# Four kinds of transfers of the mixing stage move from SyncE's queue to GpSimd's

## The chip, the cores and the metric

The kernel runs on one core of a Trainium2 chip. The metric is the device time of one execution, in microseconds; a figure for a version is the median of several executions. The engines have names of their own in the profile: PE is TensorE (PEld its weight loads), DVE is VectorE, ACT is ScalarE, POOL is GpSimd, SP is SyncE. A q behind a name (SPq, POOLq) is that engine's sequencer, which issues transfers and waits for semaphores.

## The reference, cut to what matters

One layer of a hybrid decoder, float32, for a prompt of 512 tokens and eight samples of one token each, width 1024. The two groups share all weights and are handled as 520 columns.

```
x = x + 0.5 * SwiGLU_1(rmsnorm(x))                        # d_ff 2816
h = rmsnorm(x);  z = h @ w_in                             # columns [u | q | k | v | gate_a | gate_b]
A: u -> diagonal complex SSM, 64 groups of 16 channels and 64 states -> + D u -> gelu -> sigmoid GLU
B: dilated window attention, 12 heads of 64, q and k normed per head; three head groups mixed by softmax
x = x + (sigmoid(gate_a) * A @ w_proj_a + sigmoid(gate_b) * B @ w_proj_b) @ w_out
x = x + 0.5 * SwiGLU_2(rmsnorm(x))
```

Outputs are also the SSM's last states, the new keys and values, and the samples' caches of keys and values moved on by one row.

## The kernel before

**Products.** Activations lie with channels on the 128 partitions and the 520 tokens on the columns, in two halves of 260. A weight block of 128 output channels (128 x 1024, 512 KB) is loaded by SyncE (L176) into one of two raw tiles `wr`, then split exactly into two parts: ScalarE writes the upper one (`wh`, L166), VectorE the rest (`wl`, L167), in halves of 512 columns. A product of one weight block is 8 blocks x 3 pairs of parts x 2 halves = 48 matmuls (L218, `mm`). The split runs up to three weights ahead of the products. All matmuls of products, and those of the SSM that are put between them, carry a token that fixes their order on TensorE.

**Order.** A scheduler arranges each engine's instructions by a simulation of its own; within an engine they then run strictly in order, the issues of transfers too. An issue that waits holds up what stands behind it on its engine. `dma` is SyncE's queue, `put` ScalarE's, `later` GpSimd's.

**Stages.** The first feed-forward runs to about 400 us, with the SSM's matrices made beside it; the mixing to about 835; then come the output projections and the second feed-forward. The mixing has 50 products: two blocks of queries and keys, eight blocks of `u`, ten more of queries and keys, six of values, sixteen of gates and eight of the GLU. `pace` puts a share of the other work behind each.

**The SSM in the mixing.** Each `u` block goes from PSUM through VectorE (L791, L793) into a tile `us` of four segments of 144 columns, and each segment to DRAM (`uD`, L796), where segment and channel become rows. `entry` (L665) loads a block back (`ut`, L644, two buffers), with its entry matrices (`mt<-pD`, L658, two loads, three buffers), and multiplies four pairs of groups (L672), each behind a quarter of a product. These entries begin in the fourth `u` product and need the first block then; the eighth block's are in the third product behind the `u` products. ScalarE copies the result into the states `XS` (L673). `scan` runs on VectorE (L697 to L700), and stores the last states to `out_ostate` (L724, GpSimd). `leave` (L751) loads exit matrices (`mt<-qD`) and `ut` on GpSimd, multiplies (L758 to L760), lets ScalarE copy back into `XS` (L761) and, in every second step, stores eight pieces to `yD` (L768). `y_block` loads them for the gelu (`t_G<-yD`, L1040, GpSimd).

**Norms of queries and keys.** Their 1/rms goes to DRAM (`hD`, L825); `spread` (L842) loads two rows, each repeated over 64 partitions, into one of two buffers, which lie in the attention's output tile `OB`; `normalise` (L846) multiplies on VectorE and asks for the rows two blocks on. Keys then go out on GpSimd (`out_okT`, L867).

**What else the queues hold.** SyncE also loads the samples' cached keys and values (L1061) and rows of queries (L1067). GpSimd also stores keys, values and the samples' rows, and moves the caches during the feed-forwards.

Of the kernel before, what the change touches and what calls it, by code (L numbers as in the profile page):

```python
# [21 lines left out]
NT = 520  # L22
# [6 lines left out]
CW = 144  # L29
# [5 lines left out]
# matmuls on constants in front of the first product  # L35
WARM = 2
# order of the first loads: the rows' blocks, the first two weights' halves (8..11), the third weight
# [5 lines left out]
# the scan's steps to a product of the mixing, and the products behind which the other parts' steps go:  # L43
# exit from the states, norms of queries and keys, attention, samples' scores, samples, the SSM's output
# [14 lines left out]
def build(tc, A):  # L59
# [57 lines left out]
    # what is issued inside waits for a value of the arithmetic  # L117
# [5 lines left out]
    # the moves spread over the time of the arithmetic  # L123
# [55 lines left out]
    # the first weights come in halves  # L179
# [25 lines left out]
    # the tensor engine takes these in the order given here  # L205
# [37 lines left out]
    class Norm:  # L243
# [26 lines left out]
        # a quarter of the rows on each quadrant of the partitions while 1/rms is made, then all on each,  # L270
        # through DRAM where that is soon enough
# [33 lines left out]
    def ffn(pf, xs, R, X, last_x, filler, first=(), last=False):  # L305
        first = list(first)

        # products whose rows' 1/rms is still being made leave their banks before it is there
        def product(tag, early):
            if first:  # L310
                ps = first.pop(0)
            else:
                ps = big()
                mm(ps, wnext(), xs)
            t = tmp(tag)
            if early:
                S.activation(two(t), pv(ps), AF.Copy)
                V.tensor_tensor(t, t, R, ALU.mult)
            else:
                V.tensor_tensor(two(t), pv(ps), two(R), ALU.mult)  # L320
            return t

        for pi, (m0, m1) in enumerate(PARTS):
            a = []
            for m in range(m0, m1):
                g = product("G", m < EARLY)
                s = tmp("S")
                S.activation(s, g, AF.Silu)
                u = product("T", m < EARLY)
                V.tensor_tensor(u, u, s, ALU.mult)  # L330
                a.append(split(pf, "ah", "al", u, 8))
                for _ in range(2 if m == m0 else 1):
                    move_rows(a[-1][0].bitcast(F32))
                if pi or m:
                    filler()
            for m in range(KB):
                done = pi == len(PARTS) - 1
                # the very last goes out in halves
                halves = ((0,), (1,)) if done and m == KB - 1 and last else ((0, 1),)
                w = wnext()  # L340
                for hs in halves:
                    pd, c = big(), slice(hs[0], hs[-1] + 1)
                    mm(pd, w, a, halves=hs)
                    x = two(X[m])[:, c]
                    V.scalar_tensor_tensor(x, pv(pd)[:, c], 0.5, x, op0=ALU.mult, op1=ALU.add)
                    if done:
                        last_x(m, c, x)
                if m % 2:
                    filler()

    # ================= first feed-forward, with the SSM's matrices made beside it =================
# [7 lines left out]
    # the tensor engine's clock rises with use, so it is kept busy while the first rows come  # L359
# [17 lines left out]
    # the first two products go along with the rows' arrival  # L377
# [12 lines left out]
    def ssm_build():  # L390
# [13 lines left out]
        # the skip term joins the lag kernels' first block  # L404
# [56 lines left out]
        # input factor (abar - 1) / lambda  # L461
# [47 lines left out]
        # per eight pairs of groups: entry matrices, exit matrices, lag kernels  # L509
# [5 lines left out]
        for qt in range(4):  # L515
# [15 lines left out]
            # two pairs to a transpose  # L531
# [28 lines left out]
            # a pair to each quarter of the columns  # L560
# [40 lines left out]
    # ================= mixing: one projection, then the SSM and the attention =================  # L601
# [15 lines left out]
    # queries and keys: their 1/rms comes in with the norm over each head  # L617
# [24 lines left out]
    def uload(u):  # L642
        t = smp.tile([128, 4, CW], F32, name="ut", tag="ut", bufs=2)
        later(t, uD[u])  # L644
        return t

    # block-diagonal over a pair of groups: the blocks are loaded, the zeros stay
# [16 lines left out]
    # what each chunk's input adds to the state behind it  # L664
    def entry():  # L665
        for u in range(NP // 4):
            ut, mp = uload(u), mload(pD, u, dma)
            for a in range(4):
                p = u * 4 + a
                ps = bank()  # L670
                for ri in range(2):
                    mark(T.matmul(ps[:, ri], lhsT=mp[:, a * 2 + ri], rhs=ut[:, a, 8:CW], start=True, stop=True))  # L672
                S.activation(XS[p // NH][:, :, p % NH, 9:145], ps[:, 0:2], AF.Copy)  # L673
                yield
# [3 lines left out]
    # the states in front of every chunk, for a half of the pairs: the sums of sixteen blocks of eight chunks,  # L678
    # the states in front of the blocks, then those inside
    def scan(h):  # L680
# [34 lines left out]
        # sample states  # L715
# [11 lines left out]
    # the short steps of one half go along with the wide ones of the other  # L727
# [11 lines left out]
    # a share of the scan behind every product, and of what else goes along with them  # L739
# [10 lines left out]
    # exit from the states, and the products inside a chunk  # L750
    def leave():  # L751
        for u in range(NP // 4):
# [10 lines left out]
            if u % 2 == 1:  # L763
                p = u * 4 - 4
                for g2 in range(2):
                    for t in range(4):
                        r0 = g2 * 64 + t * 16
                        dma(yD[p:p + 8, g2, :, t].rearrange("a k j -> k a j"), X[r0:r0 + 16, 0, p0 - 4:p0 + 4, 0:NC])  # L768
# [4 lines left out]
    # four segments of tokens, the samples' in front of the first and behind the last, zeros elsewhere;  # L773
    # they go to DRAM with segment and channel on the rows, two groups to a pair
# [3 lines left out]
    for m in range(KB):  # L778
# [3 lines left out]
        # the columns' halves of 260 tokens cut the third segment  # L782
# [11 lines left out]
        for s in range(4):  # L794
            o = uD[m]
            dma(bass.AP(tensor=o.tensor, offset=o.offset + s * 16 * 4 * CW, ap=[[64 * 4 * CW, 2], [CW, 64], [1, CW]]), u[:, s])  # L796
# [3 lines left out]
    # 1/rms of the rows along the partitions, in the order of the tiles and in that of all the rest  # L800
# [26 lines left out]
    # tiles of 128 tokens in their natural order; a tile's own order has every fourth token together  # L827
# [6 lines left out]
    # the first group's queries get the tokens' natural order here, its keys that of the tiles  # L834
    OB = atp.tile([128, 2, 2, 512], F32, name="OB")
    # in front of the attention its output's place serves a moved block, the norms and the samples' columns
# [5 lines left out]
    def spread(b):  # L842
        for x in range(2):
            dma(norms[b % 2][x * 64:x * 64 + 64], hD[2 * b + x:2 * b + x + 1].broadcast_to([64, NT]))
# [31 lines left out]
    # the samples' rows: to DRAM, from there to the caches  # L876
# [26 lines left out]
    # values, keys on partitions  # L903
# [24 lines left out]
    # per order of the tokens, tile and head: the negated maximum and the sum of the exponentials  # L928
# [3 lines left out]
    # the first group's queries go in the natural order, which leaves them two tiles of keys;  # L932
    # the other groups' in the order of all the rest
# [47 lines left out]
    # each order learns the other's maxima and sums; then all of a token's keys share one softmax  # L981
# [12 lines left out]
    def combine():  # L994
# [16 lines left out]
        # the values are done with, and the tokens' weights come in their place  # L1011
# [22 lines left out]
    # the SSM's output: skip term, gelu  # L1034
# [15 lines left out]
    # the samples' scores over the cached keys, beside the SSM's way out  # L1050
# [21 lines left out]
    # their softmax over all of the groups, and the values  # L1072
    def samples():
# [40 lines left out]
        # their own new rows' share  # L1114
# [4 lines left out]
        # four samples side by side, each under the weights of all of them, of which its own are kept  # L1119
# [47 lines left out]
    # gated output of the SSM branch  # L1167
# [19 lines left out]
    # the gates come back and are closed ahead of the products that they are for  # L1187
# [40 lines left out]
    # ================= second feed-forward =================  # L1228
# [27 lines left out]
# columns of a block of eight groups as (second of pair, channel, pair)  # L1256
# [97 lines left out]
```

## Time and profile before

| | |
|---|---|
| median of the runs | 1326.69 us (three runs, 1325.2 to 1327.4) |
| span of the profiled execution | 1323.7 us |
| PE busy | 1265.4 us (96%) |
| DVE busy | 755.1 us (57%) |
| ACT busy | 468.4 us (35%) |
| POOL busy | 126.7 us (10%) |
| mean granted TensorE clock | 0.981 |
| transfers on q1 (SyncE) | 145.90 MB, 36.4% of 16 engines' span |
| transfers on q0 (GpSimd) | 60.01 MB, 15.2% |

The profile is of one execution; its span runs from its first instruction to its last and is its own time as far as the profile tells it (the device time of that execution is not told apart), 3.0 us below the median of the runs. Busy time of PE is modelled at the matmuls' ends, so a busy PE is not one at its peak. Issuing a transfer counts as busy time on POOL but not on SP. GpSimd's landings are told by the profile, SyncE's only by who waits for them.

### The profile page before, as it was taken

How to read it: one execution, taken by the hardware profiler on the slowest of the kernel's cores; microseconds unless marked ns; L12 is line 12 of the kernel's file. 1: busy time of each engine (PE TensorE's matmuls, PEld its weight loads, DVE VectorE, ACT ScalarE, POOL GpSimd, SP SyncE). 2: the span in 40 equal slices, each digit the busy share in tenths (PEclk: the TensorE clock that was granted, in tenths of full speed). 3: DMA queues.
4: the chain of work that ended last, by engine and by line, in shares of the span. 5: the costliest groups of instructions: out<-in, count | busy, mean ns of one | idle time of the engine just before them, and what ended most of it. 6: DMA issues, size and time to landing. Idle time of an engine off the chain costs nothing.

```text
span 1323.7 us, 25773 instructions
## 1 busy us (share of the span) xinstructions
PE 1265.4 (96%) x10575; PEld 1240.9 (94%) x10575; DVE 755.1 (57%) x1468; ACT 468.4 (35%) x873; POOL 126.7 (10%) x211
## 2 busy tenths in 40 slices
PE   8999999999999779997679999999999999999999
PEld 7999999999999778997578899999999999999998
DVE  6794454545564239999724776776554334444442
ACT  5332233223353223342224564444333223322331
POOL 0120010001103001001221120000010001000000
PEclk9999999999999898998789999999999999999999
DMA  6665366456656445227998635546575436533332
GB/s 216 216 212 178 101 228 191 137 168 206 188 175 155 125 125 155 81 70 242 159 160 245 208 124 145 173 153 206 172 252 162 147 93 223 160 96 112 120 100 85
DMA packets 105438, 213.92 MB, mean 162 GB/s; under 512 B 45300, under 2 KB 61200, under 8 KB 104552
## 3 DMA queue, kind: packets, MB, share of 16 engines
q1 hardware_dynamic: 87064, 145.90, 36.4%
q0 software_dynamic: 7248, 60.01, 15.2%
q10 hardware_dynamic: 11008, 6.36, 2.1%
q8 instruction: 83, 1.36, 0.4%
q14 instruction: 35, 0.29, 0.1%
HBM read 188.72 MB, written 68.60 MB: 194 GB/s over the span
## 4 chain that ended last, share of the span: by engine, by line
PE 76%; DMA 11%; DVE 8%; issue 2%; SPq 1%; ACT 1%; POOL 0%; DVEq 0%; ACTq 0%; POOLq 0%
PE bigB L218 33%; PE bigA L218 28%; PE third L218 12%; DMA wr<-in_win 3%; DMA OB<-hD 2%; DVE wl L167 2%; DMA yD<-XS 2%; DMA t_G<-yD 1%; DVE t_T L698 1%; DVE t_S L697 1%; DMA mt<-qkD 1%; DMA uD<-us 1%; DVE XS L700 1%; DVE t_S L699 1%; ACT wh L166 0%
## 5 line engine op out<-in xcount | busy, mean ns | idle before, releaser
L166 ACT ACTIVATE wh<-wr 128x512 fp32r<-128x512 f32 (+2 forms) x412 | 252.7, 617 | 600.0 <-PE bigB L218 226.0
L167 DVE TENSOR_TENSOR wl<-wr,wh 128x512 fp32r<-128x512 f32 (+2 forms) x412 | 276.6, 672 | 279.6 <-ACT wh L166 275.6
L218 PE MATMUL bigB<-xh,wh 128*128 128x260 f32 (+1 forms) x1216 | 252.9, 289 | 0.3 <-ACT ks L568 0.3
L218 PE MATMUL bigB<-xh,wl 128*128 128x260 f32 (+1 forms) x1216 | 251.9, 287 | 0.0
L218 PE MATMUL bigB<-xl,wh 128*128 128x260 f32 (+1 forms) x1216 | 249.1, 286 | 0.0
L218 PEld LDWEIGHTS bigB<-xh,wl 128*128 128x128 f32 x1216 | 191.6, 191 | 2.4 <-issue 2.4
L218 PEld LDWEIGHTS bigB<-xh,wh 128*128 128x128 f32 x1216 | 190.6, 192 | 1.8 <-issue 0.8
L218 PEld LDWEIGHTS bigB<-xl,wh 128*128 128x128 f32 x1216 | 190.4, 191 | 1.1 <-issue 1.1
L218 PE MATMUL bigA<-xh,wh 128*128 128x260 f32 x704 | 143.1, 284 | 2.5 <-ACT xh L254 2.0
L218 PE MATMUL bigA<-xl,wh 128*128 128x260 f32 x704 | 142.5, 284 | 1.0 <-DVE xl L255 0.9
L218 PE MATMUL bigA<-xh,wl 128*128 128x260 f32 x704 | 142.3, 284 | 0.0
L218 PEld LDWEIGHTS bigA<-xh,wh 128*128 128x128 f32 x704 | 109.1, 190 | 4.4 <-ACT xh L254 3.4
L218 PEld LDWEIGHTS bigA<-xl,wh 128*128 128x128 f32 x704 | 108.8, 189 | 1.6 <-DVE xl L255 1.6
L218 PEld LDWEIGHTS bigA<-xh,wl 128*128 128x128 f32 x704 | 109.1, 190 | 0.2 <-DVE wl L167 0.2
L120 POOL COPY pace<-ah 1x1 f32<-1x1 f32 x48 | 36.1, 751 | 758.2 <-ACT ah L298 758.2
L218 PE MATMUL bigA<-ah,wh 128*128 128x260 f32 x352 | 71.4, 284 | 0.0
L218 PE MATMUL bigA<-al,wh 128*128 128x260 f32 x352 | 71.1, 283 | 0.0
L218 PE MATMUL bigA<-ah,wl 128*128 128x260 f32 x352 | 70.6, 282 | 0.0
L218 PE MATMUL third<-xh,wl 128*128 128x260 f32 x288 | 58.2, 283 | 0.0
L218 PE MATMUL third<-xh,wh 128*128 128x260 f32 x288 | 58.0, 282 | 0.0
L218 PE MATMUL third<-xl,wh 128*128 128x260 f32 x288 | 57.8, 282 | 0.0
L218 PEld LDWEIGHTS bigA<-ah,wh 128*128 128x128 f32 x352 | 54.2, 189 | 0.2
(384 smaller groups left out, 2038.7 us busy)
## 6 DMA issues: line engine op xcount, KB each, us to landing
out_okv<-in_kv POOLq DMA_DIRECT2D x32, 1023.5 KB, 6.3
wr<-in_wg SPq DMA_DIRECT2D x43, 512.0 KB
wr<-in_wu SPq DMA_DIRECT2D x43, 512.0 KB
wr<-in_win SPq DMA_DIRECT2D x42, 512.0 KB
wr<-in_wd SPq DMA_DIRECT2D x32, 448.0 KB
wr<-in_wd SPq DMA_DIRECT2D x16, 512.0 KB
out_okv<-in_kv POOLq DMA_DIRECT2D x8, 1022.0 KB, 5.8
ut<-uD POOLq DMA_DIRECT2D x16, 288.0 KB, 5.5
```

Source lines behind the costliest of these rows:

```text
L120: ins = G.tensor_copy(pace[0:1, 0:1], t[0:1, 0:1])
L166: S.activation(h, raw, AF.Copy)
L167: V.tensor_tensor(l, raw, h, ALU.subtract)
L218: i = T.matmul(ps[:, hf, 0:x.shape[1]], lhsT=a[:, c], rhs=x, start=k == 0 and j == 0, stop=k == n - 1 and j == 2)
L697: V.tensor_tensor(t1, w[0], x, ALU.mult)
L698: V.tensor_tensor(t2, w[1], swap(x), ALU.mult)
L699: V.tensor_tensor(t1, t1, t2, ALU.add)
L700: V.tensor_tensor(out, add, t1, ALU.add)
```

## The change

Four kinds of transfers are issued from GpSimd instead of SyncE. Their shapes, their number and what they wait for stay as they are: 16 loads of entry matrices (64 partitions x 8 pieces of 256 bytes), 32 stores of `u` (128 rows of 576 bytes each; the DRAM side's outermost dimension is 2), 32 stores of the SSM's output (16 partitions x 8 pieces of 544 bytes) and 24 broadcasts of norms (64 rows of 2080 bytes). SyncE keeps the weights, the 1/rms to DRAM, the samples' loads and the rest. The other lines of the diff take comments away and are left out here.

```
@@ entry
         for u in range(NP // 4):
-            ut, mp = uload(u), mload(pD, u, dma)
+            ut, mp = uload(u), mload(pD, u, later)
...
@@ leave
                         r0 = g2 * 64 + t * 16
-                        dma(yD[p:p + 8, g2, :, t].rearrange("a k j -> k a j"), X[r0:r0 + 16, 0, p0 - 4:p0 + 4, 0:NC])
+                        later(yD[p:p + 8, g2, :, t].rearrange("a k j -> k a j"), X[r0:r0 + 16, 0, p0 - 4:p0 + 4, 0:NC])
...
@@ the products of u
         for s in range(4):
             o = uD[m]
-            dma(bass.AP(tensor=o.tensor, offset=o.offset + s * 16 * 4 * CW, ap=[[64 * 4 * CW, 2], [CW, 64], [1, CW]]), u[:, s])
+            later(bass.AP(tensor=o.tensor, offset=o.offset + s * 16 * 4 * CW, ap=[[64 * 4 * CW, 2], [CW, 64], [1, CW]]), u[:, s])
...
@@ spread
         for x in range(2):
-            dma(norms[b % 2][x * 64:x * 64 + 64], hD[2 * b + x:2 * b + x + 1].broadcast_to([64, NT]))
+            later(norms[b % 2][x * 64:x * 64 + 64], hD[2 * b + x:2 * b + x + 1].broadcast_to([64, NT]))
```

## Rows read from the trace of the kernel before

**Rows 1.** The page's head.

```profile
span 1323.7 us, 25773 instructions
```

**Rows 2.** Stages: start:end, length, each engine's busy time (instructions), clock, DMA, GB/s.

```profile
420.00:516.00 96.00, 78.33 (x594) 75.57 (x594) 42.05 (x99) 23.66 (x53) 6.43 (x11) 0.91 0.46 135
516.00:590.00 74.00, 74.00 (x649) 71.23 (x648) 71.14 (x191) 29.74 (x61) 5.17 (x9) 1.00 0.29 84
590.00:635.00 45.00, 37.21 (x290) 36.54 (x289) 42.05 (x93) 13.07 (x30) 6.25 (x10) 0.92 0.70 202
635.00:700.00 65.00, 41.93 (x318) 40.04 (x317) 32.86 (x57) 17.62 (x40) 19.80 (x28) 0.82 0.97 171
...
850.00:1323.00 473.00, 470.54 (x3934) 470.00 (x3933) 222.21 (x352) 152.10 (x248) 23.24 (x46) 1.00 0.46 149
```

**Rows 3.** The chain that ended last, by time: start, length, what.

```profile
424.17 0.88 DVE us L791 x4
...
443.49 7.89 DMA wr<-in_win
...
845.93 5.74 PE third L218 x48
```

**Rows 4.** Timeline of SyncE's issues, 440 to 465 us.

```profile
443.49 2.54 SPq L176 DMA_DIRECT2D wr<-in_win  x1
...
446.84 6.74 SPq L796 DMA_DIRECT2D uD<-us  x4
...
457.62 7.16 SPq L796 DMA_DIRECT2D uD<-us  x4
```

**Rows 5.** Timeline of GpSimd, 455 to 515 us; in brackets idle time before.

```profile
460.86 0.54 POOL L644 DMA_DIRECT2D ut<-uD  x1 [9.65 <-DMA uD<-us]
...
507.93 1.52 POOL L658 DMA_DIRECT2D mt<-qD  x2 [2.74 <-PE s L672]
```

**Rows 6.** Issues of transfers: count, KB each, median us to landing.

```profile
ut<-uD POOLq DMA_DIRECT2D x16, 288.0 KB, 5.5
...
mt<-qD POOLq DMA_DIRECT2D x16, 192.0 KB, 5.7
...
uD<-us SPq DMA_DIRECT2D x32, 72.0 KB
...
wD<-wt POOLq DMA_DIRECT2D x1, 16.0 KB, 3.5
```

**Rows 7.** VectorE's groups by line, 420 to 516 us: busy, mean ns | idle before.

```profile
L167 DVE TENSOR_TENSOR wl<-wr,wh 128x512 fp32r<-128x512 f32 x20 | 13.7, 684 | 44.4 <-ACT wh L166 44.4
```

**Rows 8.** Timeline of TensorE: entry products, the first, two neighbours and the last.

```profile
437.08 1.25 PE L672 MATMUL s<-ut,mt 128*128 128x136 f32 x4 [5.96 <-issue]
...
446.48 0.70 PE L672 MATMUL s<-ut,mt 128*128 128x136 f32 x4
...
448.44 0.62 PE L672 MATMUL s<-ut,mt 128*128 128x136 f32 x4
...
517.36 0.62 PE L672 MATMUL s<-ut,mt 128*128 128x136 f32 x4
```

**Rows 9.** The chain again, from 594 to 700 us.

```profile
630.04 11.91 DMA OB<-hD
...
664.84 19.65 DMA t_G<-yD
```

**Rows 10.** All transfers of line 724, the stores of the last states.

```profile
DMA to landing us min/median/max: 13.7/16.7/19.3
```

**Rows 11.** Timeline of SyncE's issues: the weights about 690 us.

```profile
672.62 0.33 SPq L176 DMA_DIRECT2D wr<-in_win  x1
...
696.72 0.39 SPq L176 DMA_DIRECT2D wr<-in_win  x1
```

**Rows 12.** Timeline of TensorE, about 654 us.

```profile
654.18 0.79 PE L758 MATMUL bigB<-XS,mt 128*128 128x136 f32 x2 [9.58 <-DMA mt<-qD]
```

**Rows 13.** Timeline of GpSimd, about 650 us.

```profile
652.70 0.57 POOL L644 DMA_DIRECT2D ut<-uD  x1 [7.55 <-DMA out_ostate<-XS]
```

More of the change, by code (lines that the diff above doesn't have):

```diff
@@ L666, in entry @@
         for u in range(NP // 4):
-            ut, mp = uload(u), mload(pD, u, dma)
+            ut, mp = uload(u), mload(pD, u, later)
             for a in range(4):
@@ L767, in leave @@
                         r0 = g2 * 64 + t * 16
-                        dma(yD[p:p + 8, g2, :, t].rearrange("a k j -> k a j"), X[r0:r0 + 16, 0, p0 - 4:p0 + 4, 0:NC])
+                        later(yD[p:p + 8, g2, :, t].rearrange("a k j -> k a j"), X[r0:r0 + 16, 0, p0 - 4:p0 + 4, 0:NC])
             yield
@@ L795, in build @@
             o = uD[m]
-            dma(bass.AP(tensor=o.tensor, offset=o.offset + s * 16 * 4 * CW, ap=[[64 * 4 * CW, 2], [CW, 64], [1, CW]]), u[:, s])
+            later(bass.AP(tensor=o.tensor, offset=o.offset + s * 16 * 4 * CW, ap=[[64 * 4 * CW, 2], [CW, 64], [1, CW]]), u[:, s])
         if m > 5:
@@ L843, in spread @@
         for x in range(2):
-            dma(norms[b % 2][x * 64:x * 64 + 64], hD[2 * b + x:2 * b + x + 1].broadcast_to([64, NT]))
+            later(norms[b % 2][x * 64:x * 64 + 64], hD[2 * b + x:2 * b + x + 1].broadcast_to([64, NT]))
     def normalise(b):
```

## The prediction

> **What bounds the kernel now.** I read the table by stages first. In the second feed-forward TensorE is busy 470.54 of 473 us at full clock, so whatever the mixing gives or loses reaches the end undiminished; nothing of the change lies there [rows 1, 2]. The mixing has three poor stretches. From 420 to 516 us, while the eight u blocks are made and the entry matrices applied, TensorE is busy 78.33 of 96 us with only 594 matmuls, at a mean clock of 0.91, and no engine is near full: VectorE 42.05, ScalarE 23.66, GpSimd 6.43, the DMA engines 0.46. From 516 to 590 VectorE, with the scan, is busy 71.14 of 74 us and sets the pace. From 590 to 700 TensorE falls to 37.21 of 45 and 41.93 of 65 us, with the DMA engines at 0.70 and 0.97, though at 171 GB/s in the second part: short pieces, not bytes.
>
> Then the chain of waits: in the first stretch it runs through stores of u and through loads of weights that need 7.89 us each [rows 3]. SyncE's own timeline tells why: issuing a weight load takes 2.54 us there, and the four stores of one u block 6.74 us, the next block's beginning 457.62 - 446.84 = 10.8 us later [rows 4]. GpSimd waits for a block's stores before it loads the block back: it stands idle 9.65 us and issues, in 0.54 us, at 460.86, which is 7.3 us after SyncE was through with the stores at 453.58 [rows 4, 5]. So four stores of 72 KB each land over 7 us or more, while the one load of the same 288 KB lands in 5.5 [rows 6]; with the engines together under half busy, the stores use few of them, and weights that need all of them queue behind. VectorE's idle time before the weights' second parts is 44.4 us of those 96, all put down to ScalarE's first part, which waits for the weight [rows 7].
>
> **The change, part by part.**
> *Stores of u (32) and loads of entry matrices (16) leave SyncE.* The ceiling comes from TensorE's rows. The first entry product waits 5.96 us for u; from its start at 437.08 to that of the last at 517.36 are 31 intervals, 80.28 us. An undisturbed interval is 448.44 - 446.48 = 1.96 us, so 31 of them are 60.8. That leaves 80.3 - 60.8 = 19.5, and with the first wait 25.4 us [rows 8]. This is all that the stretch can give back.
>
> What stays: a block now goes VectorE, four stores on GpSimd (4 x 0.54 = 2.2 us, at the price of its load [rows 5]), landing, load, landing. Landing of a GpSimd store isn't shown for this size: 3.5 us for 16 KB is below it, 5.7 for a load of 192 KB in short pieces stands above; I take 4, nearer to the first, since a store is 72 KB. With 5.5 for the load [rows 6] and 0.9 for VectorE's four wide parts [rows 3], that is 12.6. The order of the matmuls leaves two whole products and a quarter, 2 x 5.74 + 1.4 = 12.9 [rows 3], for the first block, and over 15 for the others, whose products hold entries (4 x 1.96 each). So the first wait shrinks from 6 to between 0 and 2, say 1.5, and later ones vanish. I leave another 3.5 us for ScalarE and VectorE taking things in their own order. Gain 25.4 - 1.5 - 3.5 = about 20; bounds 12 (landings at 5.7 and half of the small waits left) and 25.
>
> GpSimd itself has room: seven issues a block at 0.54 to 0.76 us (the dearer is half of the 1.52 for a pair of exit loads [rows 5]) are some 4.3 us of every 7.8. Behind a wait for a block's landing it holds only the entry matrices of that block and the next block's stores, which aren't ready sooner. The gain also survives the scan: the scan is fed by the entry products, so it starts and ends earlier by the same amount, and VectorE's work after the last entry is unchanged.
>
> A page speaks against GpSimd here. VectorE is busy 42.05 of 96 us in the entry's stretch and 71.14 of 74 in the next, and the loads of u that GpSimd issues in both, sixteen with the exit's, land in 5.5 us by their median [rows 2, 6]. The Trainium skill, "DMA: Bandwidth & Descriptors", section "SWDGE vs HWDGE vs iDMA", says that GpSimd writes its descriptors into SBUF, where VectorE can lock it out in its two-port mode, while SyncE's are immune. By the trace nothing of that is seen; by the rule the loads and stores would come later by an amount that no row gives.
>
> *Norms' broadcasts (24).* They alternate with the normalising steps on VectorE over two buffers. On SyncE the last took 11.91 us to land [rows 9], amid GpSimd's stores of the samples' states, which land in 13.7 to 19.3 us [rows 10]. On GpSimd's queue the late ones go behind those same stores instead of beside them: at worst 19.3 - 11.9 = 7.4 us more, at best 2 less, since SyncE no longer holds them behind weights. Early ones are covered: VectorE is busy 42.05 of 45 us there. I take +3. Behind a late one stand, on VectorE, scan steps and the weights' second parts, and on TensorE the transposes of the samples' rows.
>
> *Stores of the SSM's output (32).* Four groups of eight, each waiting for ScalarE's copy. On SyncE the second group lies in a gap from 672.62 to 696.72 with no weight issued [rows 11]. On GpSimd eight cost 8 x 0.54 = 4.3 us, ahead of the exit's matrices and of u for the next steps; TensorE already waits 9.58 us for such a matrix at 654.18 [rows 12]. That queue is also held by transfers under way: the load of u at 652.70 waits 7.55 us for a store of states that it has nothing to do with [rows 13], and each extra transfer meets that hold sooner. Against it, weights no longer stand behind these stores. Bounds: 8 us gained (a third of the 23 that TensorE isn't busy there [rows 2]) and 2 x 9.58 = 19 lost. The rows lie nearer to a small loss, since three of the four groups come where TensorE has other products to do: +3.
>
> *Sum.* -20 + 3 + 3 = -14 us. The profiled execution's span is 1323.7 us, 3.0 below the runs' median of 1326.7; I carry the difference over to the median: 1326.7 - 14 = 1312.7, rounded to **1312 us**. If only the bounds of the terms are added, it is -25 - 2 - 8 = -35 to -12 + 7.4 + 19 = +14.
>
> **Rivals.**
> *The stores stay slow.* If the u stores run on the same few DMA engines from GpSimd too, a block still needs its 7 us and more to land, weights meet them there, and the period of 10.8 us stays. Only SyncE's issuing is relieved, by 2.54 - 0.33 = 2.2 us a weight [rows 4, 11], which the landing hides; with the 6 of the later parts the time would be about 1326.7 to 1333, say 1329. For it: the shape of the store is not changed. Against it: the same 288 KB as a GpSimd load lands in 5.5 us, and GpSimd's stores needn't share a queue with the weights.
> The page of the Trainium skill named above bears on this twice. "Issuing engines are not separate DMA queues" says that all issuers share sixteen engines and that spreading saves issue time alone, which would make this rival likely. "Why a DMA increments its semaphore by 16 and not by 1" says that the outermost dimension sets how many engines a transfer uses (here 2), with SyncE always taking the lowest and GpSimd going round, by which the rival would fall. The trace shows no single engine.
>
> *The exit pays more than the entry gains (slower).* Place: GpSimd's queue between 635 and 720 us. If each of the three groups of output stores that stand ahead of exit loads puts its 4.3 us and one landing of 5.7 between TensorE and its matrices, that is 30 us, and with 3 for the broadcasts and -20 for the entry 1326.7 + 13 = about 1340. It decides when TensorE's waits there grow by more than 17 us. For it: the queue is already held up at 652.70, and the load of y, issued at 664.84, lands 19.65 us later, with the chain behind it [rows 9]. Against it: between exit steps there are gates' products whose weights now come freely.
>
> *The exit gains too.* With weights out of the way of ScalarE's copies, a third of the 23 us comes back and the broadcasts cost nothing: 1326.7 - 20 - 8 = 1299. Against it: the long landings of the states' stores, which aren't touched, set much of that stretch.
>
> **How the numbers follow.** Forecast 0.55, stores stay slow 0.10, slower exit 0.20, gain at both ends 0.15. A difference under 0.2% (2.7 us) can't be told from none. The forecast and the last case are faster, 0.70; the slow stores split 0.06 same and 0.04 slower; slower is 0.24 with the bad exit. The likeliest case alone spans 1304 to 1322. For 8 in 10, I go down to 1297, below the double gain, and up to 1334, past the slow stores and into the milder half of the bad exit.
>
> **What would show it.** In the new profile weights from 420 to 490 us should be issued in about 0.33 us and land in 4 to 6; the first entry product should wait under 2 us; the entries should lie 2 us apart, with the last some 20 us earlier; the clock there should be granted in full. The gap on SyncE before the weight of 696.72 should be gone. The wait at 654 us for the exit's matrix tells the price of the output stores: about 13 us by my sum, over 20 by the slower rival. I am wrong if u blocks still come over ten us apart, or if the stretch from 590 to 700 us has grown by more than the first one lost.

## The result, and the profile after

The changed kernel takes 1333.49 us (median; 1333.01 to 1335.18) against 1325.95 for the kernel before: a ratio of 1.0074, with a 95% interval of 1.0051 to 1.0098. That is slower by 0.5 to 1.0%. The forecast was 1312, with a range of 1297 to 1334; the time lies at its upper edge, and on the other side of the kernel before. In what follows 0.1% is 1.3 us.

The page's head, where [rows 1] had 1323.7:

```profile
span 1331.2 us, 25769 instructions
```

The table by stages, with the columns of [rows 2]. For the fifth stage, which [rows 2] does not hold, the row of before stands in a fence of its own.

```profile
420.00:516.00 96.00, 82.61 (x658) 81.04 (x658) 49.49 (x112) 28.81 (x61) 38.89 (x53) 0.91 0.53 143
516.00:590.00 74.00, 74.00 (x647) 71.58 (x645) 73.10 (x197) 28.59 (x62) 5.29 (x10) 1.00 0.26 80
590.00:635.00 45.00, 32.45 (x258) 31.45 (x256) 42.97 (x84) 12.67 (x27) 18.95 (x32) 0.94 0.87 192
635.00:700.00 65.00, 47.54 (x351) 44.85 (x353) 26.92 (x51) 20.50 (x51) 30.94 (x50) 0.80 0.94 197
700.00:835.00 135.00, 121.88 (x1008) 112.70 (x1004) 78.65 (x135) 61.32 (x138) 22.68 (x39) 0.96 0.50 152
```

```profile
700.00:835.00 135.00, 133.12 (x1145) 123.77 (x1143) 89.72 (x151) 71.99 (x164) 19.21 (x31) 1.00 0.59 180
```

The second number of a row is TensorE's busy time, with its matmuls in brackets. From 420 to 516 us there are 64 matmuls more than before, so the entry gained, though TensorE still lacks 13 of 96 us and the clock stays at 0.91. From 590 to 635 there are 32 fewer, in the next 65 us 33 more, and from 700 to 835 there are 137 fewer. So at 700 us the changed kernel is still ahead by about what the entry gave; the gain is spent behind that, and more with it.

**The entry.** TensorE's timeline, to hold against [rows 8]: the first entry product, two later ones and the last.

```profile
437.85 1.25 PE L672 MATMUL s<-ut,mt 128*128 128x136 f32 x4 [8.18 <-DMA uD<-us]
...
465.48 0.86 PE L672 MATMUL s<-ut,mt 128*128 128x136 f32 x4 [2.69 <-DMA ut<-uD]
...
484.99 0.70 PE L672 MATMUL s<-ut,mt 128*128 128x136 f32 x4 [2.52 <-issue]
...
508.67 0.62 PE L672 MATMUL s<-ut,mt 128*128 128x136 f32 x4
```

The first still waits, 8.18 us instead of 5.96, and the entries take 508.67 - 437.85 = 70.8 us instead of 80.3. Of the ceiling of 25.4 us that is 9.5 - 2.2 = 7 us. SyncE, on the other hand, is free: its weight loads between 424 and 480 us, by their minimum, median and maximum in ns, before and now, were

```profile
L176 SPq DMA_DIRECT2D wr<-in_win x6: 1747/2227/2540, 424.4 to 474.7; - x6
```

```profile
L176 SPq DMA_DIRECT2D wr<-in_win x6: 327/328/328, 424.3 to 474.7; - x6
```

The stores of u themselves, from the view of their line (issue in ns, then the landing), and GpSimd's timeline as the first blocks pass:

```profile
L796 POOL DMA_DIRECT2D uD<-us x32: 796/808/847, 417.6 to 487.3; - x32
...
DMA to landing us min/median/max: 5.1/6.2/7.5
```

```profile
417.56 3.20 POOL L796 DMA_DIRECT2D uD<-us  x4 [0.93 <-DVE us L791]
423.33 1.58 POOL L796 DMA_DIRECT2D uD<-us  x2 [2.56 <-DVE us L791]
425.33 1.59 POOL L796 DMA_DIRECT2D uD<-us  x2 [0.42 <-issue]
429.00 1.58 POOL L796 DMA_DIRECT2D uD<-us  x2 [2.08 <-DVE us L791]
430.58 0.58 POOL L644 DMA_DIRECT2D ut<-uD  x1
```

A store costs GpSimd 0.81 us, not 0.54, and lands in 6.2 us. The first block's last store is through at 420.76, but its load, the last line, is issued at 430.58: it stands on the same queue behind the four stores of the second block and two of the third, and these wait for VectorE (the brackets of 423.33 and 429.00). It then took 7.0 us to land, so it is what ends the first wait, though the profile names a store that landed beside it. Before, with the stores on the other queue, that load went out at 431.36 as soon as they had landed, so the move brought it forward by 0.8 us only.

**The exit.** The chain of waits from 611 to 678 us, as in [rows 9]:

```profile
611.76 15.05 DMA out_ostate<-XS
...
628.46 12.44 DMA OB<-hD
...
643.35 6.26 DMA mt<-qD
...
652.10 17.09 DMA out_ostate<-XS
...
669.49 8.47 DMA t_G<-yD
```

All but 7 of these 66 us are landings of transfers from GpSimd's queue, 32 of them stores of the states, which the change does not touch. How they reach the others is seen on GpSimd's timeline (in brackets the idle time before and its releaser) and then on TensorE's, whose three longest waits from 620 to 740 us these are:

```profile
639.76 0.54 POOL L844 DMA_DIRECT2D OB<-hD  x1 [8.09 <-DMA out_ostate<-XS]
```

```profile
641.79 0.80 PE L947 MATMUL sb<-qk 64*128 64x128 f32 x4 [12.66 <-DVE qk L850]
...
686.18 3.09 PE L947 MATMUL sb<-qk 64*128 64x256 f32 x12 [8.66 <-DVE p L953]
...
710.25 2.07 PE L947 MATMUL sb<-qk 64*128 64x256 f32 x6 [6.62 <-DVE p L953]
```

A broadcast that has no use for the states waits 8.09 us for their store. It is the one before it, though, that TensorE's 12.66 us hang on: line 850 needed the broadcast issued at 628.46, and that took 12.44 us to land beside the states' stores.

This wait is not yet a loss against the kernel before, which waited 9.58 us at the same place, for the exit's matrix [rows 12], and whose first exit product came at 654.18; here it comes at 644.01. These rows part the time from 590 to 835 us at that product, first in the kernel before, then now:

```profile
590.00:654.18 64.18, 43.34 (x336) 41.98 (x335) 56.64 (x112) 17.01 (x36) 12.94 (x20) 0.85 0.79 186
654.18:835.00 180.82, 168.91 (x1412) 158.36 (x1412) 107.99 (x188) 85.67 (x197) 32.33 (x50) 0.97 0.68 180
```

```profile
590.00:644.01 54.01, 33.26 (x263) 32.00 (x261) 45.96 (x89) 12.67 (x27) 21.99 (x37) 0.87 0.89 197
644.01:835.00 190.99, 168.62 (x1349) 157.01 (x1350) 102.58 (x181) 81.82 (x188) 50.58 (x85) 0.93 0.63 164
```

Up to the product TensorE is without work for 20.8 us in both; behind it for 11.9 us before and 22.4 now. So the loss lies behind the exit's first product, where the waits of 8.66 and 6.62 us are the longest. Both end with line 953, which VectorE runs in strict order behind a round of the samples' scores (L1068), and that round waits for its rows of queries (4.71 and 5.57 us on VectorE). And on SyncE, where nothing was added, a weight comes late:

```profile
702.12 0.51 SPq L176 DMA_DIRECT2D wr<-in_win  x1
708.64 1.28 SPq L1061 DMA_DIRECT2D mt<-in_kv  x3
...
737.44 0.43 SPq L1067 DMA_DIRECT2D mt<-qkD  x1
737.91 0.43 SPq L176 DMA_DIRECT2D wr<-in_win  x1
```

Between the two weights stand four rounds of the samples' scores, each of which waits for its landing and for VectorE.

### The profile page after: what moved, and what is told of

It reads as the page before. It is cut to its first block, busy times and chain, and to the rows that moved or that the text cites. A ratio compares the mean times of both kernels' runs of the same rounds, so it can differ in the third digit from the quotient of the medians.

```text
span 1331.2 us, 25769 instructions
## 1 busy us (share of the span) xinstructions
PE 1268.5 (95%) x10575; PEld 1244.1 (93%) x10575; DVE 756.5 (57%) x1468; ACT 470.9 (35%) x873; POOL 192.8 (14%) x315
## 4 chain that ended last, share of the span: by engine, by line
PE 78%; DMA 9%; DVE 7%; issue 2%; POOL 1%; ACT 1%; SPq 0%; DVEq 0%; POOLq 0%; ACTq 0%
PE bigB L218 34%; PE bigA L218 29%; PE third L218 12%; DMA out_ostate<-XS 2%; DMA mt<-qkD 2%; DMA OB<-hD 1%; DVE wl L167 1%; DVE t_T L698 1%; DVE XS L700 1%; PE s L672 1%; DMA t_G<-yD 1%; DVE t_S L697 1%; DVE t_S L699 1%; PE sb L947 1%; DMA ut<-uD 1%
```

## The experiments

Every edit also lets the scheduler lay the order anew, so a difference of 3 us between two kernels carries little; the verdicts rest on larger ones, or on pairs that agree. The times are medians, the ratios stand against the kernel before on the same chip.

### The change in parts

Each of these makes some of the four moves and leaves the others out.

```
p_entry:  uload(u), mload(pD, u, later)      and  later(bass.AP(tensor=o.tensor, ...), u[:, s])
p_out:    later(yD[p:p + 8, g2, :, t]...)
p_norm:   later(norms[b % 2]...)
p_noout:  p_entry and p_norm
```

> Only the front half of the change: the stores of u and the loads of entry matrices go to GpSimd, the broadcasts and output stores stay on SyncE. Theory A (the entry gained 8 to 9 us and the loss arose later, from the moved output stores): the last entry product about 9 us earlier than before, and nearly all of it kept, 1316 to 1319 us. Theory B (what was gained early is lost anyway, since the later stretch is paced by the states' stores and by the samples' scores, whoever issues the rest): last entry 9 us earlier, but the end within 3 us of before.

> Only the output stores go to GpSimd. Theory A: the whole loss without the gain, 14 to 18 us slower than before (about 1341). Theory B: within 5 us of before. Rival C (the moved broadcasts make the loss): within 3 us of before.

> Only the norms' broadcasts go to GpSimd. Theory A: within 3 us of before. Rival C (late broadcasts behind the states' stores delay the transposes and all that follows): 8 to 16 us slower.

> The whole change but for the output stores, which stay on SyncE. Theory A: the entry's 8 to 9 us are kept, 1316 to 1320 us. Theory B: within 3 us of before. Rival C: slower than before by 3 to 7, as the changed kernel is.

Measured: p_entry 1320.64 us, 0.9955 [0.9935, 0.9976]; p_out 1340.65, 1.0114 [1.0083, 1.0146]; p_norm 1334.86, 1.0064 [1.0034, 1.0093]; p_noout 1328.89, 1.0017 [1.0000, 1.0035]. So the entry half gives 6 us that reach the end, the output stores alone cost 15 and the broadcasts alone 8.5. Added, that is +18; the whole change measures +10, so the two costs share some 8 us. Of the theories, B falls, since the entry's gain does reach the end, and A and C hold for a part each; p_noout, the entry's gain and the broadcasts' cost together, is where neither put it. In p_out TensorE's wait for the exit's matrix, 9.58 us in [rows 12], is little longer, and a new one of 18.44 us stands behind it, again for line 953:

```profile
654.36 0.79 PE L758 MATMUL bigB<-XS,mt 128*128 128x136 f32 x2 [10.98 <-DMA mt<-qD]
...
703.27 3.15 PE L947 MATMUL sb<-qk 64*128 64x256 f32 x12 [18.44 <-DVE p L953]
```

VectorE had stood in front of that line for a load of the samples' rows, which SyncE had issued at 666.67, 2.4 us after GpSimd issued the first of two stores of the states:

```profile
690.14 0.96 DVE L1068 TENSOR_TENSOR mt<-mt 128x768 f32<-128x768 f32 x1 [18.22 <-DMA mt<-qkD]
```

GpSimd itself waits there too. These are its waits for the states' stores from 590 to 740 us (us in total, times, longest); before, the first two were 1.9 and 7.5 us and the third was not among them.

```profile
POOL mt L658 <- DMA out_ostate<-XS: 10.2, 1, 10.2
...
POOL ut L644 <- DMA out_ostate<-XS: 8.5, 1, 8.5
...
POOL out_okv L885 <- DMA out_ostate<-XS: 6.7, 1, 6.7
```

In p_norm the longest wait is TensorE's for the normalised keys, as in the whole change, and the exit's first product follows it:

```profile
649.77 0.80 PE L947 MATMUL sb<-qk 64*128 64x128 f32 x4 [11.99 <-DVE qk L850]
650.82 0.79 PE L758 MATMUL bigB<-XS,mt 128*128 128x136 f32 x2 [0.25 <-DMA mt<-qD]
```

Here too that product comes earlier than before, by 3.4 us, so what the broadcasts cost is lost behind it; no single wait there stands out as its place.

### Which wait carries the loss: SyncE's order, the samples' rows, or the states' stores

Three edits of the changed kernel. The first gives SyncE's weights and scores a fixed order:

```
-        dma(raw[:, 0:n], ap)
+        tc.stamp_issue_order_token(dma(raw[:, 0:n], ap).ins, "loads")
...
-            dma(t[:, g * 256:(g + 1) * 256], src)
+            i = dma(t[:, g * 256:(g + 1) * 256], src)
+            if kv == 0:
+                tc.stamp_issue_order_token(i.ins, "loads")
...
-            dma(qb, sampled[0][b:b + 1].broadcast_to([128, 768]))
+            tc.stamp_issue_order_token(dma(qb, sampled[0][b:b + 1].broadcast_to([128, 768])).ins, "loads")
```

> The changed kernel, with the order of two kinds of loads on SyncE written out: weights and the samples' loads for their scores are put into the order of the program's text, so that no weight stands behind more than two rounds of scores (in the changed kernel the weight issued at 737.91 us stands behind four). Theory Q (what the changed kernel loses between 700 and 740 us is the order on SyncE that the scheduler arrived at): that weight is issued about 720 us, and the time falls from 1333.5 to 1315 to 1322. Theory T (the samples' rows reach DRAM late, behind the stores of the states on GpSimd's queue, and everything behind them waits): weights still wait for the rounds of scores, 1330 to 1338.

The second takes one store away from behind the states:

```
-        later((qkD, vD)[x].rearrange("s (b f) -> (s b) f", f=128), o)
+        (put if x == 0 else later)((qkD, vD)[x].rearrange("s (b f) -> (s b) f", f=128), o)
```

> The changed kernel, but the store of the samples' rows of queries and keys is issued from ScalarE's queue, so that it doesn't go behind the stores of the states on GpSimd's. Theory T (that store lands in 16.2 us instead of 6.2 and delays the samples' scores, and with them the weights behind them on SyncE): it lands in under 8 us, the first round of scores is 10 us earlier, and the time falls to 1318 to 1325. Theory Q (order on SyncE decides): it depends on the order that comes out; if weights still stand behind four rounds the time stays over 1328.

The third makes the states' stores short:

```
+        o9 = smp.tile([128, 2, NH, 9], F32, name="o9", tag="o9", bufs=1)
         for ri in range(2):
-            later(A["ostate"][ri][:, pr], X[:, ri, :, 136:145])
+            V.tensor_copy(o9[:, ri], X[:, ri, :, 136:145])
+            later(A["ostate"][ri][:, pr], o9[:, ri])
```

> The changed kernel, with the last states first copied by VectorE into a compact tile, so that their four stores run in rows of 576 bytes on the SBUF side instead of pieces of 36 bytes. Theory S (these stores hold the DMA engines for 13 to 19 us each, and whatever GpSimd's queue has behind them pays; the moved stores and broadcasts lose there): the stores land in under 8 us, the transfers behind them in 5 to 8, and the time falls by 12 to 20 us, to 1314 to 1321. Theory Q or T alone: the stores land faster, and the time falls by under 6 us.

Measured: a_order 1325.15 us, 1.0005 [0.9990, 1.0019]; a_tok 1332.68, 1.0067 [1.0049, 1.0085]; a_ost 1307.73, 0.9881 [0.9863, 0.9899].

The order on SyncE is worth 8 to 9 us of the changed kernel's time; that is short of the 11 to 18 that its theory asked for, and the weight in question went out at 733.48, not at 720. The late store of the samples' rows falls as a cause: it landed in 8.7 us instead of 16.2, and the load for the first round of scores went out at 662.6 instead of 672.2, yet the time stayed. That load itself was slow, as VectorE's wait for it shows, and TensorE again waited for line 953 behind the rounds:

```profile
675.26 0.96 DVE L1068 TENSOR_TENSOR mt<-mt 128x768 f32<-128x768 f32 x1 [11.00 <-DMA mt<-qkD]
```

```profile
696.29 2.07 PE L947 MATMUL sb<-qk 64*128 64x256 f32 x6 [12.55 <-DVE p L953]
```

Short stores of the states give 26 us, more than the 12 to 20 expected. Their landing (11.8/15.7/17.1 us in the changed kernel) and the stage from 635 to 700 us:

```profile
DMA to landing us min/median/max: 3.2/3.7/6.8
```

```profile
635.00:700.00 65.00, 59.58 (x444) 54.72 (x443) 38.33 (x67) 28.27 (x74) 28.15 (x49) 0.90 0.80 228
```

444 matmuls instead of 351, and neither the wait of 12.66 nor that of 8.66 us is left on TensorE's timeline; the longest there is 5.19. The same four stores move the same 288 KB; only the pieces on the SBUF side grew, from 36 to 576 bytes. Other queues gain too: of ScalarE's stores of gates (`gD`, L874), three have landings that the profile tells, 7.1, 14.4 and 16.7 us in the changed kernel and 5.4, 6.5 and 7.1 here.

### Is it the moves, or the states' stores that they stand beside?

The same edit of the states on the kernel before, on the entry half, and on each exit move alone.

```
b_ost:   before  + compact states
pe_ost:  p_entry + compact states
po_ost:  p_out   + compact states
pn_ost:  p_norm  + compact states
```

> The kernel before, with the last states copied into a compact tile ahead of their stores, so that these run in rows of 576 bytes; none of the four moves. It gives what the change costs once these stores are short: the changed kernel with them is at 1307.7. Theory S (output stores and broadcasts lose on GpSimd only because of what the states' stores do to that queue): without them the change is worth its entry half alone, 5 to 8 us, so this kernel comes to 1312 to 1316. Theory X (the two moves also cost through the order and the issues on GpSimd's queue): this kernel is as fast as the changed one with short stores or faster, 1298 to 1308.

> Stores of u and loads of entry matrices on GpSimd, output stores and broadcasts on SyncE, states stored through the compact tile. Against the changed kernel with the compact tile (1307.7) it tells what the two exit moves cost there. Theory S: within 3 us of it, 1304 to 1311. Theory X: the exit moves still cost some 10 us, so 1294 to 1300.

> The kernel before with the output stores alone on GpSimd (+15 us where the states go out in pieces of 36 bytes), and with states through the compact tile. Theory S (the stores lose only beside those pieces): within 4 us of the kernel before with the compact tile (1314.8), 1310 to 1319. Theory X (they lose by their issues and their place on GpSimd's queue): 10 us or more above it, over 1324.

> The kernel before with the broadcasts alone on GpSimd (+8.5 us where the states go out in pieces), and with states through the compact tile. Theory S: within 4 us of 1314.8, 1310 to 1319. Theory X: over 1320.

Measured: b_ost 1314.80 us, 0.9907 [0.9874, 0.9940]; pe_ost 1306.78, 0.9863 [0.9842, 0.9883]; po_ost 1311.76, 0.9866 [0.9846, 0.9886]; pn_ost 1310.11, 0.9852 [0.9833, 0.9872]. In a table, each move's effect beside the two kinds of state stores, as differences of ratios:

| | pieces of 36 bytes | rows of 576 bytes |
|---|---|---|
| entry half | -0.45% | -0.44% (pe_ost - b_ost) |
| output stores alone | +1.14% | -0.41% (po_ost - b_ost) |
| broadcasts alone | +0.64% | -0.55% (pn_ost - b_ost) |
| both exit moves on top of the entry half | +1.19% (after - p_entry) | +0.18% (a_ost - pe_ost) |

All four lie where theory S put them, and X falls. The entry half doesn't care. Both exit moves together cost 1.2% beside the pieces and nothing that can be told without them. Alone they cost nothing there either; the runs of b_ost spread from 1306.0 to 1318.4 us, so that the small gains in the second column are good to about 0.4%. The kernel before gains 0.9% too when its states go out in rows; the change had made that old fault dearer.

### Why the entry gave 7 us of its 25: shape or queue

Each store of u in two of 64 partitions; on the changed kernel with `later`, on the kernel before with `dma`:

```
-            later(bass.AP(..., ap=[[64 * 4 * CW, 2], [CW, 64], [1, CW]]), u[:, s])
+            for h in range(2):
+                later(bass.AP(tensor=o.tensor, offset=o.offset + (h * 64 + s * 16) * 4 * CW, ap=[[CW, 64], [1, CW]]), u[h * 64:h * 64 + 64, s])
```

> The changed kernel, with each store of u cut into two of 64 partitions, whose outermost dimension is 64 instead of 2: 64 issues on GpSimd instead of 32. Theory E (a store with an outermost dimension of 2 runs on two of the sixteen engines, and that keeps the stores slow from GpSimd too): the stores land in 3 to 4 us instead of 5 to 7.5, u comes a product earlier, the first entry product waits under 4 us, and the time is 4 to 8 us below the changed kernel's, 1326 to 1330. Theory I (GpSimd's time to issue is what a block costs there, 0.8 us each): twice the issues make a block's stores 2 to 3 us later, the first wait grows, and the time is 1334 to 1340.

> The kernel before with each store of u cut into two of 64 partitions, on SyncE, and nothing else. Theory E (shape, not queue): the entry's stretch goes as in the kernel with both repairs, TensorE is busy for 94 us or more of 420 to 516, and of the ceiling of 25.4 us some 15 to 27 reach the end: 1299 to 1311. If what is gained is lost to the pieces of the states behind it, as it was in the changed kernel: 1312 to 1322.

Measured: a_half 1319.02 us, 0.9968 [0.9950, 0.9987]; b_half 1302.77, 0.9801 [0.9783, 0.9819]. On the kernel before, with nothing moved, the new shape gives 26 us. For b_half, these are the stage from 420 to 516 us, the first entry product and the last, and the stores' own line (issue in ns, landing in us; on SyncE the landings of 16 of the 64 stores are told):

```profile
420.00:516.00 96.00, 96.00 (x829) 93.94 (x827) 67.31 (x158) 35.21 (x72) 11.71 (x20) 1.00 0.58 160
```

```profile
430.34 0.62 PE L672 MATMUL s<-ut,mt 128*128 128x136 f32 x4
...
490.39 0.62 PE L672 MATMUL s<-ut,mt 128*128 128x136 f32 x4
```

```profile
L797 SPq DMA_DIRECT2D uD<-us x64: 445/590/1601, 418.1 to 473.3; - x64
...
DMA to landing us min/median/max: 1.8/3.0/5.4
```

TensorE is never without work, at full clock, and the entries take 60.05 us, where the prediction counts 60.8 for 31 undisturbed intervals. Theory E holds, and it was the shape and not the queue that made the ceiling. The changed kernel with the same cut lands its stores in the same 3.0 us and gains 14, more than the 4 to 8 expected, but half of what the kernel before gains. Theory I falls: twice the issues (0.53 us each instead of 0.81) did not make the kernel slower. The first load still goes out behind the next blocks' stores, and TensorE still waits:

```profile
429.43 2.11 POOL L797 DMA_DIRECT2D uD<-us  x4 [2.50 <-DVE us L791]
431.52 0.58 POOL L644 DMA_DIRECT2D ut<-uD  x1
```

```profile
434.83 1.25 PE L672 MATMUL s<-ut,mt 128*128 128x136 f32 x4 [5.76 <-DMA ut<-uD]
```

In b_half that load went out 6.4 us earlier:

```profile
425.13 0.57 POOL L644 DMA_DIRECT2D ut<-uD  x1 [11.46 <-DMA uD<-us]
```

### Both repairs, and the square of the two halves of the change

```
b_oh:   before  + compact states + cut stores of u (all transfers where they were)
pe_oh:  b_oh + entry half on GpSimd
x_oh:   b_oh + output stores and broadcasts on GpSimd
a_oh:   the changed kernel + both repairs (all four moves)
```

> The changed kernel with both repairs: compact states and each store of u in two of 64 partitions. Their gains lie in different stretches (25.9 us after 600 us, 14.4 before), so if they add, 1331.5 - 25.9 - 14.4 = 1291, range 1289 to 1296. If what the entry gains is lost again at a later wait, 1300 to 1308.

> The kernel before with both repairs and none of the moves: the stores of u stay on SyncE, in 64 issues. Theory E (the u stores were slow by their shape, whichever queue issues them): a weight is issued in 0.33 us in the entry's stretch here too, the entry gains 12 to 18 us, and the time is within 4 us of the changed kernel with both repairs, 1288 to 1299. Theory N (the queue that the weights share is what costs): it stays 8 us or more above that kernel, over 1299.

> The entry half of the change with both repairs. Between the unchanged kernel with both (1287.9) and the changed one with both (1295.3). Theory G (64 issues at 0.8 us on GpSimd, and a block's load and entry matrices behind them, are what the entry pays there): 1294 to 1298. Theory O (the difference is the exit half's): 1286 to 1290.

> Both repairs, with output stores and broadcasts on GpSimd and the entry's transfers on SyncE: the last corner of the square. Theory S (the exit half costs nothing beside short stores): the ratio is within 0.003 of the kernel before with both repairs (0.9713), so 0.968 to 0.974, some 1284 to 1291 us. Theory X (a cost of its own in a tighter schedule): 0.976 or more.

Measured: b_oh 1287.88 us, 0.9713 [0.9698, 0.9727]; pe_oh 1298.97, 0.9780 [0.9754, 0.9807]; a_oh 1295.29, 0.9769 [0.9753, 0.9786]; x_oh 1284.35, 0.9687 [0.9664, 0.9709].

In the kernel before and in the changed one, where each repair was also run alone, the two add up nearly in full, and b_oh is at the low end of what theory E gave it. With the stores cut, the entry half, which had given 0.45%, costs 0.67% (pe_oh - b_oh) and 0.82% (a_oh - x_oh): 9 to 11 us. That is theory G's side, with pe_oh 1 us above its range; its price of 0.8 us an issue does not hold, for a cut store takes 0.53. What remains of G is the place on the queue: the first load goes out at 432.84 in pe_oh and at 425.07 in b_oh, and TensorE is busy for 87.83 us of 420 to 516 there, against 96.00. The exit half gives 0.11% (a_oh - pe_oh) and 0.26% (x_oh - b_oh), within what can be told from nothing. So two small edits beside the change are worth 38 us to the kernel before, and its entry half is best left out. x_oh is the fastest, 42 us below the kernel before, though its interval meets that of b_oh.

## Why the prediction was wrong

**The ceiling was right, the gain was not.** Of the 25.4 us read from [rows 8] I took 20, with 12 as the lower bound; the trace shows 7, the runs 6. The ceiling itself held: b_half gave 26. What failed is the step "What stays". Of the 13 us that are short, 6.7 are the first wait (8.18 us instead of 1.5) and 6.5 the entries behind it, which took 10.0 us more than the undisturbed 60.8 instead of the 3.5 that I left for them: 5.2 in the waits of 2.69 and 2.52 us, the rest at a clock of 0.92. For the first wait, three terms were too small: 0.54 us to issue a store (0.81; [rows 5] showed a load), 4 us to land it (6.2, above my bound of 5.7), and the first load, for which I counted landing alone, stood behind six stores on its new queue until 430.58. That last one is the step that I waved through with "the next block's stores, which aren't ready sooner": they are not ready, and the load behind them waits with them. For the entries I had named only ScalarE's and VectorE's own order; b_half, where they take 60.05 us with cut stores on SyncE, shows that most of it hung on the stores.

**The cause was named, and given 0.10.** In "The stores stay slow" I wrote that the blocks would need as long from GpSimd if the stores ran on few DMA engines there too. It did not come whole: blocks of stores went out some 7.7 us apart (447.02, 454.76, 462.38 on GpSimd's timeline) and not 10.8. But the landing it spoke of stayed long. I argued against it from the load of the same 288 KB, which lands in 5.5 us [rows 6]; but that load has another shape. The cut stores tell shape from queue: from either queue they land in a median of 3.0 us, against 6.2 from GpSimd uncut. No row shows how many DMA engines a store used. The Trainium skill, "DMA: Bandwidth & Descriptors", section "Why a DMA increments its semaphore by 16 and not by 1", has the slowest dimension set that number; by its rule the cut takes it from 2 to 16, and the traces agree so far as they show it, by the landings. Its section "Issuing engines are not separate DMA queues", by which spreading saves the time of issuing alone, fits too: SyncE's 2.23 us for a weight became 0.33, and 6 us reached the end.

**The exit's two terms of +3 were +8.5 and +15.** Alone, the broadcasts cost more than my upper bound of 7.4, the output stores lay inside theirs of 19. The step that failed is the path. I priced the output stores by TensorE's wait for the exit's matrix, and placed them near a small loss since it has other products then; but that wait is not where they are paid (10.98 us in p_out, 1.41 in the whole change). They are paid in VectorE's strict order: a round of the samples' scores waits for its rows, line 953 stands behind it, and TensorE waits for that, 18.44 us in p_out, 8.66 and 6.62 in the whole change. My sum has no term for the rounds of scores. The sum of the terms as measured alone is -6 + 8.5 + 15 = +18, the whole is +10: on top of the other three moves the output stores cost 7.6 us (after - p_noout) and not 15, so the two exit costs are in part the same.

**The slower rival came true in place and sign, at another price and by another cause.** I gave it 0.20 and 1340 us, as 30 us of issues and landings between TensorE and its matrices. The loss fell in that stretch, but on VectorE's order and not as issues in front of the exit's matrices, and it was 1.2% or 16 us; issues cost nothing that can be told, since the same moves beside short stores of the states are free. The row that mattered was in front of me, [rows 10], with the load held at 652.70 [rows 13] beside it: I took the states' stores for a background that "set much of that stretch", and asked for the broadcasts alone what a transfer pays beside them.

**What I said would show it.** Weights were issued in 0.33 us, as forecast. The first wait under 2 us and the full clock in the entry did not come, the last entry was 8.7 us earlier and not 20, and SyncE still has a gap between two weights, from 677.87 to 702.12. The wait at 654 us was to tell the price of the output stores, and told nothing. Nor did my sign of being wrong: from 590 to 700 us TensorE is without work for 30.9 us before and 30.0 now, and the loss came behind.

**Still open.** Whether the pieces delay other transfers more by holding up GpSimd's issues (8.09 us at 639.76) or by slowing what is under way (a broadcast landing in 12.44): both are in the rows, and no run parts them. The slowing is not GpSimd's alone: ScalarE's stores of gates took 14.4 and 16.7 us beside the pieces, and the load that p_out waits 18.22 us for was SyncE's. Why the pieces cost more once the exit's transfers are GpSimd's is therefore open. Of the loss, 8 us come back with another order on SyncE alone; how much of it would remain an effect of the states' stores was not tried.

## What to carry to other kernels

Before transfers are moved to another queue, look at what lands slowly and why: a store's shape can be the whole of its price, and then it takes that price along. A queue that holds a group of slow transfers can charge it to those that join while it is under way, so the price of a move is read from the slowest landing on the new queue and not from the time of an issue, and then from what stands in order behind whoever waits for it. And a load that was free to go as soon as its data had landed loses that freedom when the next block's stores come to stand ahead of it.

## What the runs showed of the hardware

- Four stores of 72 KB with SBUF pieces of 36 bytes landed in 11.8 to 17.1 us (13.7 to 19.3 before) and took GpSimd 1.18 us each to issue; as rows of 576 bytes they landed in 3.2 to 6.8 and took 0.56, and alone that took 0.9% off the kernel before.
- Beside those pieces, two stores from ScalarE's queue landed in 14.4 and 16.7 us; with the rows of 576 bytes, three landed in 5.4 to 7.1.
- GpSimd's issue of a 128-row store of u took 0.81 us, of half of it, 64 rows, 0.53.
- A weight's issue on SyncE took 2.23 us between uncut stores of u, in b_half 0.37 to 0.54 between cut ones (the rows between 443 and 474 us), with twice as many stores on that same queue.
